# A four-mixer kernel: the delta rules' matrices, transposes and inverses put in separate stages, and gla's v projected by channel

## The chip, the cores and the metric

The kernel runs on one core of one Trainium2 chip. The metric is the device time of one execution in microseconds (us); lower is better. Times before are the median of three runs.

## The reference

One layer with x of 2048 tokens by 1024 channels. The normed x is projected to four mixers of 256 channels (4 heads of 64), whose outputs are joined, projected back, normed and added to x.

```python
h = _rmsnorm(x, pre_norm_w[l])
proj = jnp.einsum('btd,de->bte', h, w_in[l])
p_gdn, p_rwkv, p_sc, p_gla = _split(proj, [GDN_COLS, RWKV_COLS, SC_COLS, GLA_COLS])
# gdn, in chunks of 64 tokens: a delta rule, with t_mat = a_mat + I
u = lax.linalg.triangular_solve(t_mat, v * beta[..., None], ...)
w = lax.linalg.triangular_solve(t_mat, kb * jnp.exp(g)[..., None], ...)
v_new = u_c - jnp.einsum('bhck,bhkv->bhcv', w_c, s)
o = jnp.einsum('bhck,bhkv->bhcv', q_c, s) + jnp.einsum('bhij,bhjv->bhiv', attn_c, v_new)
s = s * jnp.exp(gl_c)[..., None, None] + jnp.einsum('bhck,bhcv->bhkv', k_c, v_new)
# rwkv7: also a delta rule, token by token; shortconv: a gated causal convolution
# gla, in chunks of 64: no inverse
o = jnp.einsum('bhck,bhkv->bhcv', qe_c, s) + intra_c
s = s * jnp.exp(bl_c)[..., 0, :, None] + jnp.einsum('bhck,bhcv->bhkv', ke_c, v_c)
# and at the end
out = jnp.einsum('bte,ed->btd', y, w_out[l])
x = x + _rmsnorm(out, post_norm_w[l])
```

## The kernel before, in words

The tokens are cut into 4 blocks of 512 (`NBLK`, `BL`), a block into 4 tiles of 128 (`tt`), a tile into 2 chunks of 64 (`cp`). Two tiles make a pair, so a block has two pairs of gdn (G) and two of rwkv (R): 16 pairs in all, counted by `n`.

Matmuls of the projections take operands in a high and a low part (`hh`, `hl` for the tokens, two halves of a `w` buffer for the weights), three products for each. A weight tile of 128 columns makes 24 matmuls with 512 moving columns into a PSUM bank `pp`, of which there are two. gla's v alone is projected by token: `proj_v` holds tokens still and moves 256 columns of weights, and takes both `pp` banks at once.

A pair goes through these stages. The matrices (`gdn_mats`, `rwkv_mats`, L792 and L949) make the 64 by 64 matrices of 8 chunk-heads (`Bh`, `Bl`, the high and low part), `attn` or `M4`, and also the transposed keys and values that the chain needs (`kT`, `vT`, `BKT`, `UV`). `inverse` (L580) inverts the 8 matrices together, by four levels of two groups of matmuls in the one PSUM bank `psi`, VectorE writing `W`, `X`, `Y` and the block-diagonal `Yb` between them, then a last level and a correction; the result is `Yf`. The chain (`gdn_chain`, `rwkv_chain`, L993 and L1039) carries the state over four chunks, each a string of small matmuls in `psc` with VectorE or ScalarE between. Norm, gate and store follow (`norm`, `put`); they are off the state's path. gla has a chain of its own, without an inverse.

The order is made when the kernel is recorded. Each of `chains`, `inverses`, `prepare`, the norms of the next block and `projections` is a generator; `weave` (L229) steps those that are ready by its own count of TensorE's time and the guessed latencies in `LAT`, and takes matmuls of `projections` to fill what is left. A generator waits for named events: `("B", n)` the matrices of pair n, `("I", n)` its inverse, `("C", n)` its chain, `("T", name, blk, tt)` one tile of a chain. Before the change `prepare` waits for `("I", n - 1)` before it makes the matrices of pair n, as there is one buffer each of `Bh` and `Bl`. Within an engine the chip then keeps the recorded order. The projections of rwkv of a block wait for the chain of rwkv of the block before, `("R", blk - 1)`, and those of gla for `("L", blk - 1)`, as their buffers are single. After the last block's projections come 32 output projections (two of 512 columns for each of 16 token tiles), with nothing beside them at the end.

Of the kernel before, what the change touches and what calls it, by code (L numbers as in the profile page):

```python
# [19 lines left out]
P = 128  # L20
# [25 lines left out]
CST = {"ident": 0, "dlt": 128, "cum": 256, "msi": 384, "rst": 640, "bones": 640 + BL}  # L46
NCST = 640 + BL


def make_consts():  # L50
# [10 lines left out]
    c[:, 640:NCST] = np.arange(BL) % 64 > 0  # L61
# [3 lines left out]
    m += [-((j // (2 * s) == i // (2 * s)) & (j % (2 * s) >= s) & (i % (2 * s) < s)).astype(np.float32) for s in LEVELS]  # L65
    return c, np.concatenate([x.astype(np.float16) for x in m], 1)


def layout(inp):
# [4 lines left out]
    starts += [GLA0, GLA0 + 128, GLA0 + 512, GLA0 + 640]  # L74
# [5 lines left out]
    wv = w[:, GLA0 + 256:GLA0 + 512].reshape(KT, P, 256).transpose(1, 0, 2).reshape(P, KT * 256)  # L80
# [8 lines left out]
    for nm, key in (("w0", "rwkv_w0"), ("a0", "rwkv_a0"), ("kk", "rwkv_k_k"), ("ka", "rwkv_k_a"), ("rk", "rwkv_r_k"),  # L89
# [13 lines left out]
        "wv": wv,  # L103
# [24 lines left out]
class Ring:  # L128
# [18 lines left out]
    "M4": (512, 4), "BKT": (512, 2), "UV": (512, 2),   # L147
    "ru": (256, 2), "lu": (256, 3), "or": (256, 2),  "Yf": (64 * 8, 1), "y": (256, 1),
    "t2": (BL, 4), "gk": (16, 9), "sx": (64, 1), "dr": (16, 1), "kn": (4 * TT, 3), "rB": (256, 1), "sm": (16, 14),

    "lqk": (BL, 2), "lv": (BL, 2), "lk": (128, 1), "lgz": (2 * BL, 1), "ld": (8, 1), "lg": (BL, 2), "n32": (32, 4), "gs": (TT, 2),
# [21 lines left out]
LAT = {"gates": 6.0, "ipre": 2.0, "gates2": 1.0, "norms": 3.2, "chan": 0.9, "pool": 1.38, "decay": 2.6, "mats": 2.2, "inv0": 1.0, "inv1": 2.2,  # L173
# [4 lines left out]
def h4(t):  # L178
    return t.rearrange("p (h d) -> p h d", h=4)
# [10 lines left out]
class K:  # L190
# [60 lines left out]
    def setup(self, ctx):  # L251
# [29 lines left out]
        self.rst = g("rst", BL)  # L281
        c16 = c.tile([P, 64 * (2 + len(LEVELS))], F16, name="c16")
# [187 lines left out]
    def load_half(self, blk, wi, i):  # L470
# [4 lines left out]
        if wi == "v":  # L475
            wh, wl = (t.rearrange("p (k c) -> p k c", k=2) for t in self.load_parts(blk, (wi, i), self.a["wv"][:, i * BL:(i + 1) * BL]))
            return (wh, self.hh), (wl, self.hh), (wh, self.hl)
# [3 lines left out]
    def proj(self, blk, groups):  # L481
# [3 lines left out]
        for n, (_, tiles, _) in enumerate(groups):  # L485
            nj = range(len(tiles))
            halves = [(n, j, i) for i in range(4 if tiles[0][0] == "v" else 2) for j in nj]
# [8 lines left out]
        for n, j, i, ks in work:  # L496
# [10 lines left out]
            if first:  # L507
                pss[n, j] = self.pp() if tiles[j][0] != "v" else [self.pp() for _ in range(2)]
# [3 lines left out]
            if tiles[j][0] == "v":  # L512
                yield from self.proj_v(ps, i, pairs)
                if i == 3:
                    with self.tc.high_priority(offset=PRIO):
                        tiles[j][1](ps)
                fin += 1
                continue
# [14 lines left out]
            yield 0.0  # L533

    def proj_v(self, ps, i, pairs):

        for q, (w, h) in enumerate(pairs):
            for k in range(2):
                for t in range(TT):
                    o = 256 * (t % 2)  # L540
                    self.mm(ps[t // 2][:, o:o + 256], h[:, 2 * i + k, t * P:(t + 1) * P], w[:, k, :], start=(i + q + k + t % 2 == 0),
                            stop=(i == 3 and q == 2 and k == 1), skip_group_check=True)
            yield 0.0
# [248 lines left out]
    def gdn_mats(self, tt, Bh, Bl):  # L792
# [339 lines left out]
    def prepare(self):  # L1132

        n = 0
        for blk in range(NBLK):
            for name in "GR":
# [323 lines left out]
```

## Time and profile before

| what | before |
|---|---|
| median of 3 runs (lowest, highest) | 1380.45 us (1375.13, 1382.61) |
| the profiled execution: time, span | 1379.89 us, 1378.1 us |
| TensorE busy (PE) | 1284.7 us, 93% of the span |
| VectorE busy (DVE) | 967.7 us, 70% |
| ScalarE, GpSimd busy (ACT, POOL) | 530.2 us, 355.5 us |
| mean granted TensorE clock | 0.985 |

The span runs from the first to the last instruction; the profiled execution's time is 1.8 us longer. A busy share is a mean over stages, and a small matmul counts as busy for its whole latency, about 0.2 us, though the next one can start much earlier; so TensorE at 93% is not at 93% of its peak.

### The profile page before, as it was taken

What the parts mean: (1) busy time and instruction counts of PE and PEld (TensorE: products, weight loads), DVE (VectorE), ACT (ScalarE), POOL (GpSimd) and SP (SyncE); (2) the same over time, 40 slices, a digit from 0 to 9 for tenths busy, and PEclk for the clock granted to TensorE, in tenths of its full rate; (3) what the DMA queues carried; (4) which work ended last, traced back from release to release, by engine and by line L of the source; (5) the groups of instructions that cost most, each with busy time, mean ns of one, the idle gap of its engine ahead of it and who ended that gap; (6) DMA issues with size and microseconds to landing.
All of it is one profiled execution on the core that took longest, in us unless ns stands there. A gap on an engine that the chain in (4) does not pass through costs nothing. (4 is left out here: it accounts for less than half of the span.)

```text
span 1378.1 us, 26007 instructions
## 1 busy us (share of the span) xinstructions
PE 1284.7 (93%) x10088; PEld 982.1 (71%) x10088; DVE 967.7 (70%) x2194; ACT 530.2 (38%) x1167; POOL 355.5 (26%) x437
## 2 busy tenths in 40 slices
PE   5989988899999999999999999999998998999997
PEld 3767766767667767767777677776776776677886
DVE  5766698869876895778657977888669847743232
ACT  4663454336242431425423432453224325133221
POOL 5554444201221021101301210203111135233321
PEclk9999999999999999999999999999999999999999
DMA  8776554544244424453543335432444363233442
GB/s 283 263 258 231 206 177 146 177 152 133 82 139 146 157 89 135 146 177 105 173 146 130 130 120 174 144 110 68 127 143 145 103 198 121 89 99 116 151 151 100
DMA packets 98509, 204.63 MB, mean 148 GB/s; under 512 B 9153, under 2 KB 39249, under 8 KB 98385
## 3 DMA queue, kind: packets, MB, share of 16 engines
q1 hardware_dynamic: 98384, 202.96, 44.6%
q8 instruction: 79, 1.29, 0.4%
q14 instruction: 46, 0.37, 0.1%
HBM read 153.65 MB, written 49.28 MB: 147 GB/s over the span
## 5 line engine op out<-in xcount | busy, mean ns | idle before, releaser
L199 PE MATMUL pp<-hh,w 128*128 128x512 f32 (+1 forms) x2144 | 609.6, 408 | 7.6 <-DMA w<-parts 5.9
L199 PEld LDWEIGHTS pp<-hh,w 128*128 128x128 f32 (+1 forms) x2144 | 389.8, 190 | 92.0 <-issue 4.7
L199 PE MATMUL pp<-hl,w 128*128 128x512 f32 (+1 forms) x1088 | 323.1, 408 | 2.0 <-POOL hl L435 2.0
L199 PEld LDWEIGHTS pp<-hl,w 128*128 128x128 f32 (+1 forms) x1088 | 198.2, 190 | 45.4 <-POOL hl L435 3.8
L352 POOL TENSOR_TENSOR w<-raw,w 128x512 fp32r<-128x512 f32 (+1 forms) x102 | 129.3, 1270 | 223.6 <-ACT w L351 143.0
L351 ACT CAST w<-raw 128x512 fp32r<-128x512 f32 (+1 forms) x102 | 60.3, 593 | 130.5 <-issue 56.8
L356 POOL TENSOR_TENSOR sm<-sm,mhalf 128x4 f32<-128x4 f32 (+1 forms) x64 | 59.3, 927 | 193.4 <-DVE sm L1099 148.7
L199 PE MATMUL pp<-woh,w 128*128 128x512 f32 x256 | 71.8, 401 | 0.0
L681 DVE SCALAR_TENSOR_TENSOR pq<-pq,par,pq 128x512 f32<-128x512 f32 x72 | 59.4, 826 | 11.0 <-ACT pq L678 8.5
L605 DVE COPY Yb<-Y 64x512 f16<-64x512 f16 x160 | 55.8, 349 | 2.2
L199 PEld LDWEIGHTS <-Yb 128*128 128x128 f16 x640 | 25.2, 98 | 41.5 <-issue 22.9
L199 PEld LDWEIGHTS pp<-woh,w 128*128 128x128 f32 x256 | 47.6, 191 | 9.7
L199 PE MATMUL psi<-W,Yb 128*128 128x64 f16 x640 | 32.7, 194 | 22.3 <-DVE W L613 17.5
L618 DVE TENSOR_TENSOR X<-psi,X 128x512 f16<-128x512 f32 x64 | 43.9, 686 | 12.8 <-PE psi L199 12.5
L199 PEld LDWEIGHTS <-Bb 128*128 128x128 f16 x768 | 29.8, 99 | 29.5 <-issue 23.4
L613 DVE TENSOR_TENSOR W<-psi,c 128x512 f16<-128x512 f32 x64 | 43.8, 685 | 5.9 <-PE psi L199 5.3
L1393 DVE SCALAR_TENSOR_TENSOR pq<-pq,sm,x 128x512 f32<-128x512 f32 x32 | 24.6, 769 | 30.4 <-DMA x<-in_x 19.7
L620 DVE STREAM_TRANSPOSE Y<-X 128x512 f16<-128x512 f16 x64 | 45.2, 707 | 0.7
L199 PE MATMUL psi<-X,Bb 128*128 128x64 f16 x768 | 40.0, 195 | 6.2 <-DVE X L618 4.2
L1382 ACT ACTIVATE x<-pp 128x512 f32<-128x512 f32 x32 | 19.1, 598 | 64.1 <-PE pp L199 64.1
L847 ACT COPY pq<-pp 128x512 f32<-128x512 f32 x36 | 21.1, 586 | 53.0 <-PE pp L199 53.0
L199 PE MATMUL pp<-w,hh 128*128 128x256 f32 x256 | 36.6, 289 | 0.1
(320 smaller groups left out, 2152.4 us busy)
## 6 DMA issues: line engine op xcount, KB each, us to landing
w<-parts SPq DMA_DIRECT2D x174, 512.0 KB, 3.3
parts<-w SPq DMA_DIRECT2D x58, 512.0 KB, 4.0
raw<-in_wt SPq DMA_DIRECT2D x58, 256.0 KB, 3.2
x<-in_x SPq DMA_DIRECT2D x56, 256.0 KB, 3.0
raw<-yd SPq DMA_DIRECT2D x32, 256.0 KB, 2.9
out<-pq SPq DMA_DIRECT2D x32, 256.0 KB, 2.0
x<-in_xt SPq DMA_DIRECT2D x24, 256.0 KB, 2.9
w<-parts_v SPq DMA_DIRECT2D x12, 512.0 KB, 3.3
```

What stands on the lines that cost most here:

```text
L199: return self.nc.tensor.matmul(out, w, x, **kw)
L351: self.nc.scalar.copy(hi, src)
L352: self.nc.gpsimd.tensor_tensor(lo, src, hi.bitcast(F32), ALU.subtract)
L356: self.nc.gpsimd.tensor_tensor(dst, x, self.mhalf[:, 0:x.shape[1]], ALU.pow)
L605: nc.vector.tensor_copy(Yb[hs(c), :, hs(c)], Y[hs(c)])
L613: nc.vector.tensor_tensor(W, v(ps), m4(self.lev[lv]), ALU.mult)
L618: nc.vector.tensor_tensor(X2, v(ps), X, ALU.add)
L620: nc.vector.transpose(Y, X)
L681: nc.vector.scalar_tensor_tensor(acc, p[:, i:i + BL], self.pcol("conv", 4 * ct + i), acc, ALU.mult, ALU.add)
L847: nc.scalar.copy(p[:, 1:], ps)
L1382: nc.scalar.activation(junk, ps[i], AF.Square, accum_out=ss[:, i:i + 1])
L1393: nc.vector.scalar_tensor_tensor(o, o, r, x, ALU.mult, ALU.add)
```

## The change

The matrices of a pair and the transposed keys and values that only the chain reads are now two generators' steps: `gdn_mats` and `rwkv_mats` end with the matrices, and `gdn_more` and `rwkv_more` do the rest after them, before an event `("M", n)` for which the chain waits as well. `Bh` and `Bl` have two buffers, so that `prepare` waits for the inverse of pair n - 2 instead of n - 1. `M4` has six buffers instead of four and `attn` three instead of two; the fourth tile's matrices wait for the first tile's chain, and `more` of the second pair for the same tile of the first pair.

To make room for it, `BKT` is gone (the transposed keys are copied back over `BK`, in two copies instead of one), `t2` has three buffers instead of four, `gdn_out` shares the buffer `y` with the other outputs, and the reset mask is kept in fp16. gla's v is projected like every other tile, two tiles of 128 channels, and transposed in `gla` beside the keys, so that one copy of 384 columns takes the place of one of 128. The cut diff:

```diff
--- before.py
+++ after.py
...
+    "t2": (BL, 3), "gk": (16, 9), "sx": (64, 1), "dr": (16, 1), "kn": (4 * TT, 3), "rB": (256, 1), "sm": (16, 14),
...
+    "lqk": (BL, 2), "lv": (BL, 2), "lkv": (384, 1), "lgz": (2 * BL, 1), "ld": (8, 1), "lg": (BL, 2), "n32": (32, 4), "gs": (TT, 2),
...
-    "kq": (2 * BL, 2), "gv": (BL, 2), "ggz": (2 * BL, 1), "attn": (256, 2), "kT": (256, 4), "vT": (256, 2),
-    "gu": (256, 3), "t1": (256, 3), "og": (256, 2), "gy": (256, 1),
+    "kq": (2 * BL, 2), "gv": (BL, 2), "ggz": (2 * BL, 1), "attn": (256, 3), "kT": (256, 4), "vT": (256, 2),
+    "gu": (256, 3), "t1": (256, 3), "og": (256, 2),
...
-RINGS16 = {"Bh": 1, "Bl": 1, "W": 1, "X": 2, "Y": 1}
+RINGS16 = {"Bh": 2, "Bl": 2, "W": 1, "X": 2, "Y": 1}
...
-        kT, vT = g["kT"][tt], self.R["vT"]()
-        nc.vector.tensor_tensor(h4(kT), h4(kT), bc(g["ke"]), ALU.mult)
-        ps = self.psa()
-        for pr in range(2):
-            self.tr(ps[:, pr * P:(pr + 1) * P], g["v"][pr][:, tt * P:(tt + 1) * P], self.ident)
-        nc.vector.tensor_tensor(h4(vT), h4(ps[:, 0:256]), bc(g["kv"]), ALU.mult)
...
-        return dict(attn=h4(attn), kT=kT, vT=vT)
+        return dict(attn=h4(attn))
+
+    def gdn_more(self, tt, m):
+
+        nc = self.nc
+        g = self.g
+        bc = lambda s: s[:, 4 * tt:4 * tt + 4].unsqueeze(2).to_broadcast([P, 4, 64])
+        kT, vT = g["kT"][tt], self.R["vT"]()
...
+        m.update(kT=kT, vT=vT)
+        yield 0.0
...
-            en, ak = self.t2(), self.t2()
+            en, ak, kk = self.t2(), add[:, pr, :], lw
...
-            kk = self.t2()
...
+        yield 0.0
+        return dict(M4=M4)
...
+    def rwkv_more(self, tt, m):
+
...
         ps = self.psa()
...
-        bt = self.R["BKT"]()
-        nc.scalar.copy(bt, ps)
+        for pr, bd in enumerate(bds):
...
+        for pr, bd in enumerate(bds):
+            nc.scalar.copy(bd, ps[:, 2 * P * pr:2 * P * pr + 2 * P].rearrange("p (c x) -> p c x", c=2))
...
-        return dict(M4=M4, bt=bt, uv=uv)
+        m.update(bt=bds, uv=uv)
...
-                o = (2 * cp + h // 2) * P + 64 * (h % 2)
-                self.mm(pC[hs(h % 2), hs(h // 2)], bt[:, o:o + 64], uv[:, cp, hs(h)], start=True, stop=True)
+                self.mm(pC[hs(h % 2), hs(h // 2)], bt[h // 2][:, cp, hs(h % 2)], uv[:, cp, hs(h)], start=True, stop=True)
...
-        y = self.R["gy"]()
+        y = self.R["y"]()
...
-                    if n:
-                        yield "I", n - 1
+
+                    if n > 1:
+                        yield "I", n - 2
                     B, ms = [self.R16[x]() for x in ("Bh", "Bl")], []
+                    mats, more = (self.gdn_mats, self.gdn_more) if name == "G" else (self.rwkv_mats, self.rwkv_more)
+                    for i in range(2):
+                        tt = 2 * pair + i
+                        if tt == 3:
+                            yield "T", name, blk, 0
+                        m = yield from mats(tt, *(t[:, 4 * i:4 * i + 4, :] for t in B))
+                        ms.append(m)
+                    self.mats[n] = ms, B
+                    self.done("B", n, lat=LAT["mats"])
                     for i in range(2):
                         if pair:
                             yield "T", name, blk, i
-                        m = yield from (self.gdn_mats if name == "G" else self.rwkv_mats)(2 * pair + i, *(t[:, 4 * i:4 * i + 4, :] for t in B))
-                        ms.append(m)
-                    self.mats[n] = ms, B
-                    self.done("B", n, lat=LAT["mats"])
+                        yield from more(2 * pair + i, ms[i])
+                    self.done("M", n, lat=LAT["more"])
                     n += 1
...
                         yield "I", n
+                        yield "M", n
                         ms, Y = self.mats.pop(n)
...
-        todo = [(None, ((WT_GLA + i, lambda ps, t=t: nc.scalar.copy(t, ps)),), None) for i, t in enumerate((qf, kf))]
...
-        def fv(ps):
-            for t, p in zip(v, ps):
-                nc.scalar.copy(t, p)
-        todo.append((None, (("v", fv),), None))
+        todo = [(None, ((WT_GLA + i, lambda ps, t=t: nc.scalar.copy(t, ps)),), None) for i, t in enumerate([qf, kf] + v)]
...
-        at, ke, vt = u1(), self.R["lk"](), L["v"][tt // 2][:, 256 * (tt % 2):256 * (tt % 2) + 256]
+        at, kv = u1(), self.R["lkv"]()
+        ke, vt = kv[:, 0:P], kv[:, P:]
...
         pt = self.psa()
-        self.tr(pt[:, 0:P], L["ed"][:, ts], self.ident)
-        nc.scalar.copy(ke, pt[:, 0:P])
+        for i, t in enumerate([L["ed"]] + L["v"]):
+            self.tr(pt[:, i * P:(i + 1) * P], t[:, ts], self.ident)
+        nc.scalar.copy(kv, pt[:, 0:3 * P])
         yield LAT["gA"]
...
```

On TensorE, in the last tile of block 0's rwkv chain, from its first chunk to its second (`Sr`, `ru` and `UV` are operands of the chain's matmuls, `Yf` the inverse, `BKT` or `BK` the transposed keys, `qbd` and `lg` gla's, `or` an output, `pp` the projections), the rows before, word for word:

```order
L199 MATMUL pp<-hh,w_160 128x512 x3
L199 MATMUL pp<-hh,w_158 128x512
L199 MATMUL psc<-ru_80,Yf_87 64x64 x4
L199 MATMUL pp<-hh,w_158 128x512 x3
L199 MATMUL pp<-hl,w_158 128x512 x2
L199 MATMUL psc<-UV_79,BKT_77 64x64 x4
L203 MATMUL psa<-cst,or_85 128x128 x2
L199 MATMUL psa<-qbd,lqk_123 64x256 x2
L203 MATMUL psa<-cst,lg_129 128x128
L199 MATMUL pp<-hl,w_158 128x512
L199 MATMUL psc<-Sr,AR_63 128x128
L199 MATMUL psc<-Sr,AR_64 128x128
```

and in the same tile now:

```order
L197 MATMUL pp<-hh,w_161 128x512 x4
L197 MATMUL pp<-hh,w_159 128x512 x4
L197 MATMUL psc<-ru_80,Yf_87 64x64 x4
L197 MATMUL pp<-hl,w_159 128x512 x4
L197 MATMUL pp<-hh,w_159 128x512 x4
L197 MATMUL pp<-hh,w_160 128x512
L197 MATMUL psc<-UV_79,BK_65 64x64 x2
L197 MATMUL psc<-UV_79,BK_66 64x64 x2
L197 MATMUL pp<-hh,w_160 128x512 x3
L197 MATMUL pp<-hl,w_160 128x512 x4
L197 MATMUL psc<-Sr,AR_63 128x128
L197 MATMUL psc<-Sr,AR_64 128x128
```

Between the chain's matmuls with `Sr` and `ru`, `ru` and `UV`, `UV` and `Sr` stood 4, 5 and 1 projection matmuls, and in the last place gla's first matmuls; now 8, 9 and 7 projection matmuls stand there.

On VectorE, where the inverse of the first pair of block 0 begins (`Bb`, `Y`, `X`, `Yb`, `W` are the inverse's; `t` and `attn` a gdn pair's matrices; `AR` and `BK` the rwkv projections), before:

```order
L591 COPY Bb_151<-Bh_145 64x8x64 x2
L598 TENSOR_TENSOR Y_150<-Bh_145,c_203 128x512
L801 TENSOR_TENSOR t_196<-cst,gk_93 128x256
L599 TENSOR_TENSOR Y_150<-Y_150,c_203 128x512
L802 TENSOR_TENSOR t_198<-cst,gk_97 128x256
L601 STREAM_TRANSPOSE X_148<-Y_150 128x512
L605 COPY Yb_152<-Y_150 64x8x64 x2
L381 TENSOR_TENSOR sm_118<-sm_117 128x4
L382 TENSOR_SCALAR sm_118<-sm_118 128x4
L613 TENSOR_TENSOR W_147<-psi,c_203 128x512
L852 SCALAR_TENSOR_TENSOR AR_63<-pq_138,par,pq_139 128x4x128
```

and now:

```order
L569 COPY Bb_152<-Bh_144 64x8x64 x2
L576 TENSOR_TENSOR Y_151<-Bh_144,c_204 128x512
L577 TENSOR_TENSOR Y_151<-Y_151,c_204 128x512
L785 TENSOR_TENSOR t_199<-t_199,t_200 128x256
L579 STREAM_TRANSPOSE X_149<-Y_151 128x512
L583 COPY Yb_153<-Y_151 64x8x64 x2
L591 TENSOR_TENSOR W_148<-psi,c_204 128x512
L798 TENSOR_TENSOR t_200<-psa,t_198 128x2x64
L799 TENSOR_TENSOR attn_188<-psa,t_199 128x2x64
L798 TENSOR_TENSOR t_200<-psa,t_198 128x2x64
L799 TENSOR_TENSOR attn_188<-psa,t_199 128x2x64
L596 TENSOR_TENSOR X_150<-psi,X_149 128x512
```

The second pair's matrices (`t`, `attn`), which before came after this inverse was written out, now stand between its first steps; the vT of both tiles comes in before the inverse begins. Counted in VectorE's instructions from the start, the four inverses of block 0 are written out after 167, 308, 408 and 553 before, and after 173, 314, 401 and 489 now.

## Rows read from the trace of the kernel before

**Rows 1.** The page: busy us by engine, and its TensorE and clock slices.
```profile
PE 1284.7 (93%) x10088; PEld 982.1 (71%) x10088; DVE 967.7 (70%) x2194; ACT 530.2 (38%) x1167; POOL 355.5 (26%) x437
PE   5989988899999999999999999999998998999997
```

**Rows 2.** The last-ending chain in order of time: start us, us, what.
```profile
1273.60 97.06 PE pp L199 x428
```

**Rows 3.** Stretches, projection matmuls alone: busy us (count), clock, DMA share, GB/s.
```profile
100.00:1262.00 1162.00, 824.54 (x3247) 0.99 0.43 140
180.00:260.00 80.00, 51.37 (x239) 0.96 0.45 155
340.00:420.00 80.00, 45.78 (x151) 0.98 0.38 118
680.00:900.00 220.00, 166.73 (x680) 0.99 0.43 141
```

**Rows 4.** Same stretches, all engines: PE, PEld, DVE, ACT, POOL, clock, DMA.
```profile
100.00:1262.00 1162.00, 1096.51 (x9249) 831.58 (x9249) 866.94 (x1991) 447.25 (x987) 268.47 (x342) 0.99 0.43 140
180.00:260.00 80.00, 67.61 (x579) 54.62 (x578) 68.08 (x132) 33.40 (x71) 33.77 (x29) 0.96 0.45 155
340.00:420.00 80.00, 77.78 (x831) 56.15 (x830) 63.97 (x177) 30.84 (x80) 16.42 (x24) 0.98 0.38 118
680.00:900.00 220.00, 211.17 (x1705) 162.47 (x1703) 166.84 (x369) 76.17 (x162) 31.96 (x52) 0.99 0.43 141
```

**Rows 5.** TensorE's waits: us in total, times, longest.
```profile
PE psi L199 <- DVE W L613: 17.5, 17, 4.8
PE psi L199 <- DVE X L618: 4.2, 5, 2.1
PE psa L199 <- DVE t L801: 3.5, 1, 3.5
PE psi L199 <- DVE Yb L605: 2.5, 4, 0.9
PE psi L199 <- DVE W L626: 2.1, 3, 1.0
PE psi L199 <- DVE X L601: 1.9, 2, 1.5
```

**Rows 6.** Groups by line: operation, count, busy, mean ns, idle before.
```profile
L199 PE MATMUL pp<-w,hh 128*128 128x256 f32 x256 | 36.6, 289 | 0.1
L199 PE MATMUL pp<-w,hl 128*128 128x256 f32 x128 | 18.6, 288 | 0.0
L983 ACT COPY BKT<-psa 128x512 f32<-128x512 f32 x16 | 9.3, 582 | 1.1 <-PE psa L203 0.8
L989 ACT COPY UV<-psa 64x256 f32<-64x256 f32 x32 | 11.7, 366 | 2.0 <-PE psa L203 1.6
```

**Rows 7.** TensorE's timeline: start, us, then line, operation, tiles, shapes, count.
```profile
537.60 1.08 PE L199 MATMUL pp<-hh,w 128*128 128x512 f32 x4
538.61 0.45 PE L199 MATMUL psc<-ru,Yf 64*64 64x64 f32 x8
...
553.58 1.12 PE L199 MATMUL pp<-w,hh 128*128 128x256 f32 x8
554.63 0.45 PE L199 MATMUL psc<-ru,Yf 64*64 64x64 f32 x8
...
918.48 1.09 PE L203 MATMUL psa<-cst,kq 128*128 128x128 f32 x8
919.50 0.39 PE L199 MATMUL psi<-X,Bb 128*128 128x64 f16 x8
```

**Rows 8.** Tiles: ns min, median, max of the 128-column copy and of `Yb`.
```profile
L1289 ACT COPY lk<-psa x16: 242/265/266, 372.9 to 1252.8; 128x128 f32<-128x128 f32 x16
L605 DVE COPY Yb<-Y x160: 242/291/1411, 100.6 to 1185.3; 64x512 f16<-64x512 f16 x160
```

**Rows 9.** Timelines of one stall of block 0: VectorE, GpSimd, TensorE; then the clock.
```profile
182.60 2.77 DVE L605 COPY Yb<-Y 64x512 f16<-64x512 f16 x2
187.15 0.68 DVE L613 TENSOR_TENSOR W<-psi,c 128x512 f16<-128x512 f32 x1
...
182.08 1.73 POOL L352 TENSOR_TENSOR S<-radd,S 128x512 fp32r<-128x512 f32 x1
...
187.88 0.58 PE L199 MATMUL psi<-W,Yb 128*128 128x64 f16 x8 [4.78 <-DVE W L613]
...
185.00:195.00 10.00, 7.12 (x38) 5.82 (x39) 8.92 (x16) 4.82 (x8) 1.52 (x2) 0.66 0.30 105
```

More of the change, by code (lines that the diff above doesn't have):

```diff
@@ L73, in layout @@
     starts += [SC0 + P * i for i in range(8)]
-    starts += [GLA0, GLA0 + 128, GLA0 + 512, GLA0 + 640]
+    starts += [GLA0 + P * i for i in range(6)]
     tiles = [w[:, s:s + P].reshape(KT, P, P).transpose(1, 0, 2).reshape(P, KT * P) for s in starts]
@@ L280, in setup @@
         self.strict, self.incl = self.msi[:, 0, 0:64], self.msi[:, 0, 64:128]
-        self.rst = g("rst", BL)
-        c16 = c.tile([P, 64 * (2 + len(LEVELS))], F16, name="c16")
+        c16 = c.tile([P, 64 * (2 + len(LEVELS)) + BL], F16, name="c16")
+        self.rst = c16[:, 64 * (2 + len(LEVELS)):]
         par = c.tile([P, NPAR], F32, name="par")
@@ L486, in proj @@
             nj = range(len(tiles))
-            halves = [(n, j, i) for i in range(4 if tiles[0][0] == "v" else 2) for j in nj]
+            halves = [(n, j, i) for i in range(2) for j in nj]
             order += halves
@@ L507, in proj @@
             if first:
-                pss[n, j] = self.pp() if tiles[j][0] != "v" else [self.pp() for _ in range(2)]
+                pss[n, j] = self.pp()
             if n == 0:
@@ L532, in proj @@
                     self.done("P", blk, after, lat=2.5)
[L533 to L542, printed above, removed]
             yield 0.0
@@ L829, in gdn_mats @@
         nc.gpsimd.tensor_tensor(Bl, h4(B32), Bh, ALU.subtract)
-        return dict(attn=h4(attn), kT=kT, vT=vT)
+        return dict(attn=h4(attn))
[4 more added lines that the diff above has]
+        kT, vT = g["kT"][tt], self.R["vT"]()
+        nc.vector.tensor_tensor(h4(kT), h4(kT), bc(g["ke"]), ALU.mult)
+        ps = self.psa()
+        for pr in range(2):
+            self.tr(ps[:, pr * P:(pr + 1) * P], g["v"][pr][:, tt * P:(tt + 1) * P], self.ident)
+        nc.vector.tensor_tensor(h4(vT), h4(ps[:, 0:256]), bc(g["kv"]), ALU.mult)
+        m.update(kT=kT, vT=vT)
+        yield 0.0
     def rwkv_proj(self):
@@ L971, in rwkv_mats @@
         nc.gpsimd.tensor_tensor(Bl, h4(B32), Bh, ALU.subtract)
-        for pr in range(2):
-            bd = BK[pr][:, 2 * tt:2 * tt + 2, :]
+        yield 0.0
+        return dict(M4=M4)
+    def rwkv_more(self, tt, m):
+        nc = self.nc
+        r = self.r
+        BK = r["BK"]
+        bds = [BK[pr][:, 2 * tt:2 * tt + 2, :] for pr in range(2)]
+        for pr, bd in enumerate(bds):
             for c in range(2):
@@ L977, in rwkv_mats @@
         ps = self.psa()
-        for cp in range(2):
-            for pr in range(2):
-                o = (2 * cp + pr) * P
-                self.tr(ps[:, o:o + P], BK[pr][:, 2 * tt + cp, :], self.ident)
-        bt = self.R["BKT"]()
-        nc.scalar.copy(bt, ps)
+        for pr, bd in enumerate(bds):
+            for cp in range(2):
+                o = (2 * pr + cp) * P
+                self.tr(ps[:, o:o + P], bd[:, cp], self.ident)
+        for pr, bd in enumerate(bds):
+            nc.scalar.copy(bd, ps[:, 2 * P * pr:2 * P * pr + 2 * P].rearrange("p (c x) -> p c x", c=2))
         ps = self.psa()
```

28 lines of the change are left out of this document (7 added, 21 removed).

## The prediction

> **What bounds the kernel now.** I read the page first: TensorE is busy 93% of the span, VectorE 70%, the other two far less, and the slices show no long stretch in which TensorE is free except at the very start [rows 1]. The chain of waits says the same from the other end: followed back from the last instruction it is 97.06 us of 428 projection matmuls and nothing else [rows 2], 0.227 us each. That is the price of such a matmul when nothing interrupts it. So the kernel is bound by TensorE's queue, and a stage is worth what it adds to that queue: its matmuls, and the time in which the queue stands still or crawls.
>
> How much of the middle is crawl? Between 100 and 1262 us the projections have 3247 matmuls [rows 3], 384 of them gla's v with 256 columns (counted below). All matmuls there are 9249 [rows 4], so 6002 are small ones. 2863 at 0.227 are 650 us, the 384 at 0.131 (below) 50 us; 462 us are left for the small ones, 77 ns each, with all waits and switches in it. The same sum by stage: 67 ns in 340 to 420 us (151 projections, 680 small), 73 ns in 680 to 900 us (584 projections, 96 of v, 1025 small), 103 ns in 180 to 260 us (143, 96 and 340) [rows 3, 4]. In that last stage a gdn chain, an inverse, rwkv's preparation and block 0's weight splitting meet; VectorE is busy 68.08 of 80 us there, more than in any other of these stages. So the price of a small matmul moves with how late VectorE is, not with how few projections are left: the stage poorest in projections, 340 to 420 us, is the cheapest.
>
> The waits by name: TensorE waits mostly for the inverse's VectorE steps. Six kinds of wait stand in [rows 5]; the five of them that belong to the inverse (`W`, `X`, `Yb`) sum to 28.2 us, and the wait for `t`, the first step of a gdn pair's matrices, is 3.5 us, once.
>
> **The change, part by part.** The sum is made against the profiled execution: span 1378.1 us, time 1379.9 us, 0.5 us under the median of 1380.45.
>
> gla's v. Before: 384 matmuls of 256 columns [rows 6]; eight of them take 1.05 us from 553.58 to the next row's 554.63, 0.131 us each, 50.3 us in all [rows 7]. Now: 192 matmuls of 512 columns. Four take 1.01 us between chain steps [rows 7], 0.2525 us each, 48.5 us; at the undisturbed 0.227 they would be 43.6 us. I take the price in the midst of the chains: **-1.8 us**, bound -6.7 us. The weights' bytes and loads stay the same, four halves a block.
>
> Transposes of v in gla: two more for each of 16 tiles, 32. Eight transposes of that shape take 1.02 us [rows 7], 0.1275 us each: **+4.1 us** on TensorE's queue. The copy behind them grows from 128 to 384 columns: 0.265 us for 128 [rows 8], 0.582 us for 512 [rows 6], so about 0.48, 0.2 us more, 16 times, 3.4 us. ScalarE is busy 530.2 us of the span [rows 1], and the mask of `at` on VectorE runs beside it; I take 0, bound +3.4 us.
>
> `BKT`'s copy in two: 0.582 us becomes about two of 0.366 [rows 6], 0.15 us more for each of 16 tiles, on ScalarE and now before the event `M`, not before the inverse: 0, bound +2.4 us. The new wait for `M` has only the chain's own next matmul behind it. If the chain comes first, that matmul stops TensorE's whole queue. But `M` is recorded while the inverse still has levels to go, so I take 0.
>
> Shorter rings: `y` shared by all outputs, `t2` with three buffers. The cover is the distance between outputs, as tiles of one chain follow each other through four chunk steps, and an output's write is one of 16 for each mixer in the whole run. I take 0; if a write met an unfinished store, the VectorE queue would stand behind it. Fp16 mask: the same scan, 0.
>
> The decoupling itself. It removes no instruction. It lets a pair's matrices stand between another inverse's steps, takes the scaling of `kT`, the copies and transposes of `vT`, `BK`, `UV` out of what the inverse waits for, and, as the order of VectorE shows, brings the fourth inverse of block 0 forward by 64 instructions (553 to 489). At VectorE's mean of 0.44 us (967.7 us over 2194 [rows 1]) that is 28 us of VectorE work. But the first three come out after 173, 314 and 401, against 167, 308 and 408: nothing is won there. What is won is filling: in the last tile of rwkv 8, 9 and 7 projection matmuls stand where 4, 5 and 1 stood, each worth about 0.25 us.
>
> What is that worth? Below: nothing, if the filling only moves from one place to another, as every projection put here is missing elsewhere. Above: all 6002 small matmuls at the best stage's 67 ns instead of 77, 57 us. Between: at the price of 680 to 900 us, 73 ns, it would be 23 us. By the waits: 28.2 us of the inverse and 3.5 us for `t`. I take the whole of the 3.5, since the matrices no longer wait for the inverse ahead, and two fifths of the 28.2, as one inverse in four moves clearly and the others have another pair's matrices around them: 11.4. Together **-15 us**, which is 2.5 ns for each small matmul, well inside the bound.
>
> The sum: 1379.9 - 1.8 + 4.1 - 15 = 1367.2. **I predict 1367 us.**
>
> **Rivals.** A measurement of this kernel tells about 0.5%, 6.9 us, from no change: faster is under 1373.5, slower over 1387.4.
>
> *More is won.* If all waits of the inverse and for `t` go, 31.7 us, the time is 1379.9 - 1.8 + 4.1 - 31.7 = 1350.5. With them some of the low clock would go: after the stall of 4.78 us at 183 us, the granted clock of 185 to 195 us is 0.66 [rows 9], that is, part of this stretch ran at 1.2 GHz and the rest at 2.4; a third of 10 us, 3.4 us, was lost to one stall. Five of that size would give 1350.5 - 17 = 1334. For it speaks that the waits are many and short; against it, that VectorE has no instruction less. The Trainium skill, "TensorE: Matmul & The Clock Gate", section "HAM oscillation — how this bites in real kernels", has it that idle gaps of TensorE are paid twice, by the gap and by a slow clock after it. The trace agrees at this stall, with its 0.66.
>
> *Nothing is won.* VectorE does the same work in the same total, 967.7 us [rows 1], and where the stages meet it was already late. The filling moves and the waits move with it. Then only v and the transposes count: 1379.9 + 2.3 = 1382. For it speaks that the cheapest stage was the one with fewest projections, and that three inverses of four come no earlier.
>
> *Slower.* Three things now run together, a chain, an inverse and another pair's matrices, and VectorE becomes the bound where it was near it. The place is the middle of each block, from the second gdn pair to the first rwkv pair, as in 180 to 260 us, with VectorE 0.85 busy [rows 4]. One wait there took 4.78 us: two `Yb` copies took 2.77 us instead of twice the median 0.291 [rows 8], and `W` came last behind them; GpSimd ran a 1.73 us subtraction at the time [rows 9]. If each of the 16 inverses loses 2.5 us more, 40 us, less the 12.7 won in the sum above, the time is 1379.9 + 40 - 12.7 = 1407; at 2 us it is 1399. It decides from (12.7 + 6.9) / 16 = 1.2 us for each inverse. Against it: only block 0 splits weights on GpSimd, which is busy 31.96 of 220 us later on [rows 4]. The Trainium skill, "SBUF — State Buffer", section "Who interferes with whom", says that a copy of VectorE in a two-port mode and a GpSimd instruction exclude each other for a whole instruction, which speaks against putting more of the inverse beside GpSimd's work. The stretched `Yb` copies agree with it.
>
> **How the numbers follow.** The forecast, 1358 to 1373 us, has 0.40. More won, under 1358, has 0.15. Nothing won, 1373.5 to 1387, has 0.27: the order's evidence for three inverses of four. Slower has 0.18. So faster 0.55, same 0.27, slower 0.18. The range leaves out the outer half of both end cases: from 1346 (the 1350.5 of all waits gone, with v at its bound of -6.7) to 1390, just past the bound of no change with the copies' 3.4 and 2.4 us on the path (1388). The likeliest case alone goes from 1358 to 1373.
>
> **What the profile will show.** If the steps are right: TensorE's waits for `W`, `X` and `Yb` sum to some 17 us instead of 28.2, the wait for `t` is gone, TensorE's busy time falls less than the span does, and the undisturbed run of projections at the end is longer than 97 us by the filling that was not needed earlier, with the same 0.227 us each. 192 more projection matmuls of 512 columns and 32 more transposes of `lv` stand there, with ScalarE's copy at 0.45 to 0.5 us. It is wrong if the waits for VectorE keep their sum under other names (chain steps `gu`, `UV`, `Sg`), which gives 1382, or if TensorE waits for the tiles of `more`, or for a `y` whose store has not landed. It is wrong on the far side if VectorE is over 0.95 busy in the middle of every block.

## The result and the profile after

The changed kernel takes 1388.0 us (median of 20 runs, 1376.9 to 1394.8), the kernel before 1379.1 us (20 runs beside it, 1373.7 to 1383.1). The ratio is 1.0061, 95% interval 1.0046 to 1.0077: 0.6% slower, where 1.0% faster was forecast (1367 of 1380.45). The profiled execution took 1384.26 us, its span is 1382.4 us. Ratios below leave out runs over 1.5% above the fastest of their kernel, which are three of e2's twelve (with them e2 is at 1.0041).

The page's engines and TensorE's slices, as [rows 1]:

```profile
PE 1283.9 (93%) x9928; PEld 976.0 (71%) x9928; DVE 955.6 (69%) x2194; ACT 529.4 (38%) x1181; POOL 355.0 (26%) x437
PE   5979878999989999999999898999998998999997
```

The last link of the last-ending chain (start, us, what, count), as [rows 2]:

```profile
1257.94 117.00 PE pp L197 x516
```

TensorE is busy as long as before and idle 5 us longer (1382.4 - 1283.9 = 98.5 against 93.4). The undisturbed run of projections at the end grew from 97 to 117 us, at the same 0.227 us each. So the middle needed less filling, as forecast, but it ended only 15.7 us sooner (1257.94 against 1273.60) for the 20 us of filling that it left to the end. Stretches, projections alone (as [rows 3]), then all engines (as [rows 4]):

```profile
100.00:1262.00 1162.00, 820.43 (x3045) 0.99 0.43 140
...
100.00:1262.00 1162.00, 1095.93 (x9083) 825.96 (x9083) 857.41 (x1997) 445.81 (x998) 268.38 (x342) 0.99 0.43 140
180.00:260.00 80.00, 68.76 (x577) 52.40 (x575) 72.14 (x150) 33.53 (x76) 30.91 (x26) 0.91 0.39 136
```

The small matmuls cost (1162 - 3045 x 0.227) / 6038 = 78.0 ns each, against 77: the 2.5 ns that the forecast wanted are not there. In 180 to 260 us VectorE is busy 72 of 80 us, more than before, and the clock fell to 0.91. TensorE's waits, as [rows 5] (us in total, times, longest):

```profile
PE psi L197 <- DVE W L591: 20.8, 18, 2.9
PE psi L197 <- DVE X L579: 9.3, 7, 1.9
PE psa L197 <- DVE t L779: 3.8, 2, 2.8
PE psa L197 <- DVE W L604: 3.5, 4, 1.4
PE psi L197 <- DVE Yb L583: 3.4, 6, 1.3
PE psi L197 <- DVE X L596: 2.1, 4, 1.3
PE psi L197 <- DVE X L613: 1.4, 4, 0.4
```

The six kinds of the inverse sum to 40.5 us; all such kinds of before, two short ones more than [rows 5] shows, sum to 30.4. The wait for `t` is still there. X L579 is the inverse's start (X L601 before, 1.9 us): TensorE now comes to it before VectorE has. These waits are not what the time follows: in the run e1 below, 1.2% faster, the waits of the inverse still sum to 35.9 us, the two largest being

```profile
PE psi L197 <- DVE W L591: 19.9, 17, 4.1
PE psi L197 <- DVE X L579: 6.6, 5, 2.1
```

The timelines of VectorE at the end of the same inverse, that of block 3's second gdn pair, show what the overlap does to an inverse. First the changed kernel, then e1, in which a pair's matrices are held for the inverse ahead:

```profile
1070.61 0.67 DVE L613 TENSOR_TENSOR X<-psi,X 128x512 f16<-128x512 f32 x1
...
1073.00 0.68 DVE L949 TENSOR_TENSOR M<-psa,cst 128x512 f32<-128x512 f32 x1
...
1074.37 0.67 DVE L627 TENSOR_TENSOR W<-X,psi 128x512 f16<-128x512 f16 x1
...
1075.05 1.18 DVE L953 TENSOR_TENSOR rB<-M,kn 64x128 f32<-64x128 f32 x4
1076.25 1.29 DVE L949 TENSOR_TENSOR M<-psa,cst 128x512 f32<-128x512 f32 x2
1077.53 1.19 DVE L953 TENSOR_TENSOR rB<-M,kn 64x128 f32<-64x128 f32 x4
...
1079.35 0.68 DVE L636 TENSOR_TENSOR Yf<-psi,Y 128x512 f32<-128x512 f32 x1
```

```profile
1050.46 0.68 DVE L613 TENSOR_TENSOR X<-psi,X 128x512 f16<-128x512 f32 x1
...
1052.94 0.68 DVE L627 TENSOR_TENSOR W<-X,psi 128x512 f16<-128x512 f16 x1
...
1053.62 0.68 DVE L949 TENSOR_TENSOR M<-psa,cst 128x512 f32<-128x512 f32 x1
...
1055.00 0.69 DVE L636 TENSOR_TENSOR Yf<-psi,Y 128x512 f32<-128x512 f32 x1 [0.62 <-PE psi L197]
1055.68 0.58 DVE L953 TENSOR_TENSOR rB<-M,kn 64x128 f32<-64x128 f32 x2
```

In the changed kernel the first rwkv pair's `M` and `rB` stand between the correction's last steps, and from X to Yf it takes 8.7 us. In e1, with one `M` ahead of `Yf`, it takes 4.5, and there VectorE waits for TensorE (0.62 us, in brackets); in the kernel before it takes 4.8. Over all 16 inverses, from TensorE's first matmul to the end of `Yf`, the mean is 36.7 us in the changed kernel, 35.1 in e1 and 35.3 before.

**The clock differs too.** Each run has its granted clock. Over its 20 runs the changed kernel's mean is 0.9828; over 34 runs beside the first four experiments the kernel before has 0.9893. Time multiplied by clock, which takes one lost per cent of clock as one lost per cent of time, is 1362.8 us for the one and 1362.9 for the other. By that measure the whole loss is clock, but it takes too much off. By a straight line through the changed kernel's runs 0.01 of clock goes with 11.2 us, through those of the kernel before with 8.3, not 14 (in other kernels with anything from 0, e11, to 14, e1); by the first two 2 to 4 of the 9 us are left at one and the same clock, and the two profiled executions, both at 0.985, differ by 4.4 us. So some 5 to 7 of the 9 us go with the clock, and whether the clock or the order behind it is the cause is not shown. The experiments are told in both measures. The kernel before, taken again beside each group of them (e1 to e4, e5 to e8, e9 to e12, e13 to e15, e16 and e17), has 1362.9, 1360.3, 1361.3, 1360.8 and 1355.5 us in time x clock (1360.5 without one run that took 1372.87 us at 0.951), so that a difference of under 3 us between groups says nothing.

### The profile page after: what moved, and what is told of

The parts are those of the page before. It is cut to its first block, busy times and chain, and to the rows that moved or that the text cites. A ratio compares the mean times of both kernels' runs of the same rounds, so it can differ in the third digit from the quotient of the medians.

```text
span 1382.4 us, 25708 instructions
## 1 busy us (share of the span) xinstructions
PE 1283.9 (93%) x9928; PEld 976.0 (71%) x9928; DVE 955.6 (69%) x2194; ACT 529.4 (38%) x1181; POOL 355.0 (26%) x437
## 4 chain that ended last, share of the span: by engine, by line
PE 52%; DVE 18%; issue 4%; POOL 3%; ACT 3%; DMA 2%; SPq 0%; POOLq 0%; ACTq 0%; DVEq 0%
PE pp L197 39%; PE psc L197 6%; PE psa L197 3%; PE psi L197 2%; PE psa L201 2%; POOL sm L354 2%; DVE Yb L583 1%; DMA x<-in_xt 1%; DVE X L596 1%; DVE W L591 1%; DVE Y L598 1%; DVE t L879 0%; DVE AR L895 0%; DVE M L949 0%; DVE og L1023 0%
## 5 line engine op out<-in xcount | busy, mean ns | idle before, releaser
L197 PE MATMUL pp<-hh,w 128*128 128x512 f32 (+1 forms) x2272 | 646.0, 408 | 5.3 <-DMA w<-parts 3.2
L197 PEld LDWEIGHTS pp<-hh,w 128*128 128x128 f32 (+1 forms) x2272 | 412.0, 190 | 90.6 <-DMA w<-parts 4.1
L197 PE MATMUL pp<-hl,w 128*128 128x512 f32 (+1 forms) x1152 | 342.7, 410 | 2.0 <-POOL hl L433 2.0
L197 PEld LDWEIGHTS pp<-hl,w 128*128 128x128 f32 (+1 forms) x1152 | 210.8, 191 | 47.7 <-POOL hl L433 3.8
L1009 ACT COPY gu<-psc 64x128 f32<-64x128 f32 x64 | 16.6, 259 | 58.7 <-PE psc L197 57.4
## 6 DMA issues: line engine op xcount, KB each, us to landing
raw<-in_wt SPq DMA_DIRECT2D x62, 256.0 KB, 3.1
x<-in_x SPq DMA_DIRECT2D x56, 256.0 KB, 3.0
raw<-yd SPq DMA_DIRECT2D x32, 256.0 KB, 2.9
out<-pq SPq DMA_DIRECT2D x32, 256.0 KB, 2.3
x<-in_xt SPq DMA_DIRECT2D x24, 256.0 KB, 3.2
```

Of the source, the lines that this page charges most:

```text
L197: return self.nc.tensor.matmul(out, w, x, **kw)
```

## The experiments

Kernels against before, 4 to 12 compared runs each (the changed kernel 20; time x clock of before from the first group):

| kernel | ratio, 95% interval | mean clock | time x clock |
|---|---|---|---|
| before | 1 | 0.9893 | 1362.9 |
| changed | 1.0061 [1.0046, 1.0077] | 0.9828 | 1362.8 |
| e1 hold all | 0.9941 [0.9914, 0.9968] | 0.9882 | 1353.4 |
| e2 hold first rwkv pair | 1.0018 [0.9990, 1.0046] | 0.9887 | 1364.0 |
| e3 changed, v by token | 1.0053 [1.0034, 1.0071] | 0.9825 | 1360.9 |
| e4 before, v by channel | 1.0011 [0.9992, 1.0029] | 0.9857 | 1358.9 |
| e5 rest first | 1.0021 [1.0005, 1.0037] | 0.9884 | 1363.3 |
| e6 hold all, rest first | 1.0024 [1.0006, 1.0041] | 0.9794 | 1351.7 |
| e7 hold all, v by token | 0.9899 [0.9865, 0.9934] | 0.9905 | 1351.4 |
| e8 hold second gdn pair | 1.0074 [1.0049, 1.0099] | 0.9797 | 1358.8 |
| e9 e7, waiting for the chain | 1.0015 [0.9996, 1.0035] | 0.9853 | 1359.0 |
| e10 changed, more slack | 1.0108 [1.0077, 1.0139] | 0.9780 | 1360.9 |
| e11 e7, more slack | 0.9957 [0.9940, 0.9973] | 0.9861 | 1351.2 |
| e12 hold second rwkv pair | 1.0053 [1.0035, 1.0070] | 0.9849 | 1362.2 |
| e13, e14 pads, misplaced | 1.0292, 1.0287 | 0.976, 0.977 | 1381.1, 1382.2 |
| e15 e7, one wait less | 1.0003 [0.9993, 1.0014] | 0.9842 | 1354.9 |
| e16 e7, pads in the inverse | 1.0122 [1.0099, 1.0144] | 0.9868 | 1375.0 |
| e17 e7, pads behind it | 1.0093 [1.0067, 1.0120] | 0.9777 | 1359.3 |

**e1: the overlap undone.**

```diff
-                    if n > 1:
-                        yield "I", n - 2
+                    if n:
+                        yield "I", n - 1
```

> The changed kernel with one edit: a pair's matrices wait for the inverse just ahead again, as in the kernel before, so no matrices stand between the steps of another inverse. The split of matrices and the rest, the rings, and v by channel stay. Theory A, the bunch (in the middle of each block the second gdn pair's inverse, the first rwkv pair's matrices and a chain now fall on VectorE together, and TensorE waits): the loss of 8.9 us (ratio 1.0061) goes, down to the sum of v and the transposes, 1.000 to 1.002 of before; the stretches without projections behind the second gdn inverse, 12 to 14 us in each block, go too. Theory B, v by channel is the loss (384 matmuls of 256 columns against 192 of 512 and 32 transposes): the time stays at 1.005 to 1.007. Theory C, the moved rest (the copies and transposes behind the event M) is the loss: it stays at 1.005 or above.

Theory A's direction, and more than its size: not 1.000 but 0.9941. The overlap costs 1.2% of the time, 16.5 us (9.4 us in time x clock), and what is left of the change wins 0.6%. The inverses of block 0 start at 103.5, 163.2, 225.2 and 282.3 us; with the overlap at 103.6, 162.8, 219.8 and 282.2. So matrices that are ready sooner start one inverse of these four sooner, by 5 us, and that one also ends later, at 262.5 instead of 256.0 us. The time is lost from one block to the next: the fourth inverse of block 0 ends at 316.7 us with the overlap and 317.3 without, but the first of block 1 starts at 400.3 instead of 390.8, that of block 2 at 694.9 instead of 674.2, that of block 3 at 976.8 instead of 956.4. From the first start to the last end in a block the overlap saves 1 to 6 us, but fewer projections go in there (516 instead of 544 in block 0) and have to be made behind it. Theory A's other sign did not come: around the second gdn inverse the longest gap between projections is 7.1 to 8.8 us with the overlap and still 5.4 to 8.1 without.

**e2, e8, e12: one pair of each block held** (the same line, for one pair only).

> The changed kernel with one edit: only the first rwkv pair of each block waits for the inverse just ahead of it; the other pairs keep the overlap. Theory A, the bunch in the middle of each block: this one wait takes the bunch away and the wins at the block's ends remain, so the time is 0.995 to 1.000 of before, under that of the kernel in which all pairs wait. If the overlap costs the same at each pair, it is a quarter of the way: 1.0045. Theory B and C (v by channel, the moved rest): 1.005 to 1.007, as the changed kernel.

> The changed kernel in which only the second gdn pair of each block waits for the inverse ahead of it; the other three keep the overlap. If the loss is shared by the four pairs evenly, a quarter of 1.2% comes back: 1.003. If it sits in the inverse of the second gdn pair (its inverses last 43 to 51 us with the overlap and 40 to 48 without): this pair's matrices are not the ones that stand in that inverse, they stand in the first pair's, so nothing comes back, 1.005 to 1.007. If it sits between the two gdn pairs, 0.997 to 1.000.

> The changed kernel in which only the second rwkv pair of each block waits for the inverse ahead. Holding the first rwkv pair brought nothing in time multiplied by clock (1363 us as 1363), holding the second gdn pair 4 us (1359), holding all four 9.4 us (1353). If the shares add, the second rwkv pair and the first gdn pair have the 5.9 us left: here 1357 to 1360 us in time multiplied by clock, 1.000 to 1.005 of before in time. If only all together count, 1361 to 1363, 1.005 to 1.008.

In time x clock, holding the first rwkv pair, where I had looked for the whole loss, brings nothing (1364.0), the second rwkv pair 0.6 us, the second gdn pair 4.0; all together 9.4. In time, 0.4% and 0.1% come back in the first two and nothing in the third, whose clock is lowest; e12 is what was expected if only all together count. So none of these three places holds the loss, and Theory A's "middle of each block" is too narrow; the first gdn pair was not held alone.

**e3, e4: v by channel.** e3 is the changed kernel with the old `proj_v`, `wv` and the 128-column copy; e4 is the kernel before with the new ones.

> The changed kernel with gla's v projected by token as before (384 matmuls of 256 columns, no transposes of v, the copy of 128 columns). Theory A, the bunch: by the sum of the prediction, 2.3 us less than the changed kernel, 1.004 to 1.0045 of before; at most 4 us less. Theory B, v by channel is the loss: 1.000 or below.

> The kernel before with gla's v by channel alone (192 matmuls of 512 columns, 32 transposes of v, the copy of 384 columns, the shared y). Theory A: the sum of the prediction, +2.3 us, 1.0017 of before; between 0.9985 (the matmuls at 0.227 us each) and 1.004 (the copy on the path too). Theory B: the whole loss, 1.006.

Theory B is out: undone in the changed kernel, v gives back 0.1% in time, 1.9 us in time x clock. Alone in the kernel before it changes the time by 0.1%, inside its interval. The sum's +2.3 fits but is not resolved: in time x clock v by channel costs 1.9 us in the one kernel and saves 4.0 in the other (1358.9 against 1362.9 beside it).

**e5, e6: the split undone,** with the overlap and without: the rest of a pair comes ahead of the event that the inverse waits for.

```diff
-                    self.done("B", n, lat=LAT["mats"])
                     for i in range(2):
                         if pair:
                             yield "T", name, blk, i
                         yield from more(2 * pair + i, ms[i])
+                    self.done("B", n, lat=LAT["mats"])
```

> The changed kernel with the split undone and the overlap kept: the rest of a pair (scaling and transposes of kT, vT, BK, UV and their copies) is issued before the event B that the inverse waits for, as before, and not after it. Theory D (what the first runs leave: the split wins, the overlap loses; the inverses are paced by the chains and so do not use matrices that are ready sooner): the split's win of 7 to 9 us is gone and the overlap's loss is still there, 1.010 to 1.014 of before. Rival E (split and overlap only hurt together, as the rest of one pair then falls into the inverse of another): 0.998 to 1.003.

> The changed kernel with split and overlap both undone; v by channel, the rings of the change and the order of the transposes stay. Theory D: nothing is left of win or loss, 0.999 to 1.003, as the kernel before with v by channel (1.0011). If the rings or the transposes' new form count, it departs from that by over 0.3%.

e6 came as Theory D said, e5 did not: in time the overlap costs nothing without the split (1.0021 and 1.0024) and 1.2% with it. That is Rival E by the ratios. In time x clock it is no interaction: the overlap costs 11.6 us without the split (1363.3 and 1351.7) and 9.4 with it. The two views differ by the clock, 0.9794 in e6 and 0.9884 in e5, which by that measure is 28 and 16 us of 1380; the times are 1380.1 and 1379.3. No run here says which view is right.

**e7: the split alone, v by token.** The edits of e1 and e3.

> Split alone: the changed kernel with the overlap undone (each pair's matrices wait for the inverse ahead) and gla's v by token as before. Theory D: the split alone wins 0.6%, and v counts by at most 0.1% either way: 0.992 to 0.996 of before. By the sum of the prediction v by token saves 2.3 us more: 0.9925. If v by channel is what won in the run that holds all pairs, this one is back at 0.998 to 1.001.

0.9899, the lowest ratio here, 1.0% under the kernel before and a little under Theory D's range; its interval overlaps e1's. v by channel is not what won in e1.

**e9: e7, waiting for the chain again.**

```diff
-                        if tt == 3:
-                            yield "T", name, blk, 0
+                        if pair:
+                            yield "T", name, blk, i
```

> The split alone (each pair's matrices wait for the inverse ahead, v by token: 0.9899 of before), in which a second pair's matrices wait for the chain again as before, its first tile for the chain's first tile and its second for the second; the change has only its second tile wait for the first. Theory F (the win is that the inverse of a second pair no longer stands behind the chain of the first): its inverses start some 15 us later in each block, and the win goes, 0.998 to 1.002. Rival G (the win is that the inverse waits for less work, the rest being issued after B): it stays at 0.988 to 0.993.

Theory F: the win goes, 1.0015 (7.6 us in time x clock, the rest clock). The second inverse of block 0 starts at 176.5 instead of 163.1 us, the fourth at 316.9 instead of 283.3. By this run, what won was that a second pair's inverse does not stand behind the chain of the first; e15 below goes against it. In e6, where the rest waits for the chain and holds the inverse, the time is back at 1.0024 too, though not time x clock.

**e10, e11: more slack,** in the changed kernel and in e7.

```diff
-"ipre": 2.0, ... "inv0": 1.0, "inv1": 2.2,
+"ipre": 3.0, ... "inv0": 2.0, "inv1": 3.2,
```

> The changed kernel with three numbers of the planner's table larger by 1 us (ipre 2 to 3, inv0 1 to 2, inv1 2.2 to 3.2): it takes an inverse's steps to be ready later, and puts more projections between them. Theory H (with another pair's matrices between an inverse's steps, VectorE's answer comes later than the table says; TensorE reaches the next step too soon and stands): the waits for W, X and Yb fall from 40 us to under 20, and the time to 0.993 to 1.000. Rival I (VectorE is the bound in the middle of the blocks, so TensorE stands whatever is put there): the waits keep over 30 us, the inverses end later, and the time stays at 1.006 to 1.012.

> The same three numbers in the kernel with the split alone and v by token (0.9899 of before). It is the control for the run above: if the numbers were too small without the overlap too, this gains as much as that one, to 0.980 to 0.985; by theory H alone, with no other pair's matrices between the steps, little is to be had and each inverse comes later, 0.988 to 0.994.

The waits fell nearly as Theory H said, to 22.5 us and not under 20; the time did what Rival I said, so neither holds. The waits of e10:

```profile
PE psi L197 <- DVE W L591: 9.0, 8, 2.7
PE psi L197 <- DVE W L604: 5.6, 3, 3.8
PE psi L197 <- DVE X L579: 2.6, 3, 2.1
PE psi L197 <- DVE W L627: 2.5, 1, 2.5
PE psi L197 <- DVE X L613: 1.9, 2, 1.0
PE psi L197 <- DVE X L596: 0.9, 1, 0.9
```

Time x clock falls by 1.9 us only, while the time rises by 0.5%. In e7 the slack moves time x clock by 0.2 us and the time by 0.6%, outside the range expected. So the sum of TensorE's waits in the inverse is no measure of what they cost: projections put there are missing elsewhere (the run of them at the end falls from 516 to 428), and an inverse takes 7 to 8 us longer in the mean.

**e13, e14, e16, e17: VectorE's price, inside the inverse and behind it.** 12 idle multiplications for each pair, between the inverse's steps or ahead of the next pair's matrices. In e13 and e14 they read only their own spare tile:

> The split alone with v by token (0.9899 of before, 1351 us in time multiplied by clock) with idle work on VectorE added between the steps of each inverse: 12 multiplications of a spare tile of 256 columns by itself, 0.42 to 0.45 us each, 5.2 us for each of 16 inverses, about what a pair's matrices take on VectorE. Nothing reads the tile. Theory J (VectorE being late between an inverse's steps is what the overlap costs): 8 to 14 us more in time multiplied by clock, 1359 to 1365, and 0.996 to 1.004 in time. Rival L (the price is not VectorE's but lies in the order of TensorE's or ScalarE's work): at most 3 us more, 0.989 to 0.994.

> The same 12 multiplications for each pair, six ahead of each tile's matrices, which come behind the inverse and beside the chain's first steps. Theory J: little, 0 to 4 us more in time multiplied by clock, 0.989 to 0.994. Rival K (VectorE's sum counts, wherever it stands): as much as the run above. Rival L: as little as the run above.

Both put them into the first block. VectorE's slices on the page of e7, without them:

```profile
DVE  5776799697765997777668885876669967543323
```

of e13:

```profile
DVE  8999999899776699687865996867669967633322
```

and of e14:

```profile
DVE  8999999998776698687865996777659967543222
```

So these runs say nothing on the place. In e16 and e17 each reads a tile of its place:

```diff
             yield LAT["inv0"]
+            self.spare(1, W[:, 0:4, :].rearrange("p u i -> p (u i)"))
...
             yield LAT["inv0"] if lv == 3 else LAT["inv1"]
+            self.spare(2, Y[:, 0:4, :].rearrange("p u i -> p (u i)"))
```

> The split alone with v by token (0.9899 of before, 1351 us in time multiplied by clock) with 12 idle multiplications of 256 columns on VectorE between the steps of each inverse, one behind each W and two behind each Y, reading that tile, so that they stay there; nothing reads what they write. About 0.43 us each, 5.2 us for an inverse, as much as a pair's matrices take on VectorE, 83 us in all. Theory J (VectorE's lateness between an inverse's steps is what the overlap costs): 8 to 14 us more in time multiplied by clock, 1359 to 1365, 0.996 to 1.004 in time. Rival K (VectorE's sum counts, wherever it stands; the front-loaded runs lost 30 us in that measure): 20 us more or above, 1.005 to 1.03. Rival L (not VectorE): at most 3 us more.

> The same 12 multiplications, for 15 of the 16 pairs, six ahead of each tile's matrices, reading the inverse just ended, so that they stand behind it and beside the chain's first steps. Theory J: 0 to 4 us more in time multiplied by clock, 0.989 to 0.994. Rival K: as much as the run above. Rival L: as little as the run above.

The groups by line of e16 (count, busy us, mean ns, idle before):

```profile
L1188 DVE TENSOR_TENSOR pad<-Y 128x256 f32<-128x256 f16 x128 | 65.4, 511 | 1.5
L1188 DVE TENSOR_TENSOR pad<-W 128x256 f32<-128x256 f16 x64 | 31.2, 488 | 0.9
```

and of e17:

```profile
L1189 DVE TENSOR_TENSOR pad<-Yf 128x256 f32<-128x256 f32 x180 | 86.5, 481 | 3.4
```

In time, the work costs 2.2% inside the inverse and 1.9% behind it, 0.32 and 0.31 us for each us of it: that is Rival K. In time x clock, 96.6 us of VectorE's work inside the inverse cost 23.6 us (0.24 us for each), 86.5 us behind it 7.9 (0.09): Theory J has the order right there, and both sizes are above its ranges. The traces bear out that much of it: an inverse takes 38.3 us in the mean in e16 and 35.4 in e17, against 35.3 in e7. A pair's matrices are about 5 us of VectorE (by e7's groups of `t` and `attn`, or of `M` and `rB`); moved from behind the inverse into it, 16 times 5 at 0.24 - 0.09 are 12 us, an estimate in time x clock, where the overlap costs 9 to 12. In time the place is worth nothing in these two runs, so that VectorE's lateness accounts for the overlap's 1.2% only if the clock is counted apart; that is argued, not shown.

**e15: one wait less.** e7 without `yield "T"` for gdn and a fourth buffer of `attn`.

> The split alone with v by token, in which a second gdn pair's second tile doesn't wait for the chain's first tile either (a fourth buffer for attn); the rwkv pairs keep that wait. By theory F (an inverse that doesn't stand behind the chain is the win) the four inverses of the second gdn pairs come some 2 to 5 us sooner: 0.985 to 0.990. If the chain's first tile is done by then anyway, no change, 0.988 to 0.993.

A miss: 1.0003 instead of 0.9899, 3.5 us of it in time x clock. The inverses of the second gdn pairs, counted from the first of their block, come 1.3 to 2.3 us sooner in three blocks and 2.7 us later in the first. One wait less thus loses in time nearly as much as e9's wait put back, so that part of e9's loss may be the order and its clock, and Theory F is supported, not shown; why e15 loses, no run here shows.

## Why the prediction was wrong

**gla's v and the transposes, +2.3:** nothing speaks against it, but it is too small to be resolved. The wider copy takes 0.478 us, as worked out (0.48); e3 and e4 put v within 0.1% in time, inside their intervals.

**Rings, `y`, the mask, the wait for `M` at nothing:** no wait of TensorE for the tiles behind `M` (`vT`, `UV`, `BK`) or for `y` is among its longer ones, and e6, which keeps all of these, is at 1.0024.

**The decoupling, -15: the step that failed.** I took it from the inverse's waits, two fifths of 28.2 us (11.3, not the 11.4 written) and the whole of 3.5, and took both halves of the decoupling for one. With the 2.3 of v taken off the 8.9 us of loss, the term measures +6.6. The runs show two edits of opposite sign. The split, with which a second pair need not wait for the chain's tiles, brings 0.6 to 1.0% (e1, e7), gone when the wait is put back (e9). The overlap, by which a pair's matrices may stand beside the inverse ahead, costs 1.2% on top of the split (e1 against the changed kernel); without the split it costs nothing in time (e5, e6). Through what the overlap costs that, VectorE or the clock or both, stays open. The 64 instructions by which the fourth inverse comes forward were read rightly, but they belong to the first half: in block 0 its end comes at 316.7 us instead of 354.8, and at 317.3 without the overlap. And the waits were the wrong ledger: e10 nearly halves them and wins nothing, and e1 beats the kernel before with more of them (35.9 us against 30.4).

**"Nothing is won"** named what happened to the waits: they moved and grew. 1382 is near the result by accident; two effects of 8 to 17 us lie under it. That the stated range, to 1390, takes in 1388 is luck of the same kind: its upper end came from this rival.

**"Slower"** came nearest: VectorE is late where an inverse and another pair's matrices meet. By its formula the result, 8.9 us over before, is (8.9 + 12.7) / 16 = 1.35 us for each inverse, not 2 to 2.5, just past the 1.2 from which it decides; the inverses of the traces are 1.4 us longer than before, 1.6 longer than in e1. That each such us costs a us is still its assumption. Its sign, VectorE over 0.95 busy in the middle of every block, came in two of four: 490 to 520 and 780 to 810 us, in blocks 1 and 2 (clock, DMA share and GB/s follow; the third line is the kernel before, which has such a stretch too):

```profile
490.00:520.00 30.00, 29.11 (x73) 0.94 0.23 78
780.00:810.00 30.00, 29.24 (x71) 1.00 0.24 80
...
470.00:500.00 30.00, 29.18 (x69) 1.00 0.32 102
```

Its 0.18 was too low: that VectorE has no instruction less and that three inverses of four come no earlier stood in the prediction, and speak for it as much as for "nothing is won".

**The clock** stood in the prediction only as an extra of "more is won". One stretch shows it near the crowded VectorE: three pieces around the end of block 3's second inverse, all engines, then clock:

```profile
1058.00:1068.00 10.00, 9.08 (x56) 7.11 (x54) 9.80 (x17) 3.11 (x5) 3.07 (x2) 1.00 0.53 184
1068.00:1078.00 10.00, 8.32 (x102) 6.47 (x101) 9.85 (x31) 4.85 (x14) 2.12 (x3) 0.81 0.24 80
1078.00:1088.00 10.00, 9.35 (x69) 7.40 (x68) 7.43 (x18) 6.00 (x17) 2.27 (x2) 0.85 0.17 52
```

Between 1068 and 1074 us VectorE is full, nearly all matmuls are small and TensorE stands 1.7 us in gaps of under 0.6 us, all at a granted clock of 1.00; from 1074 to 1080 TensorE is busy throughout and the clock is 0.50 to 0.54, which is 1.2 GHz. The Trainium skill, "TensorE: Matmul & The Clock Gate", section "HAM oscillation — how this bites in real kernels", has idle gaps paid a second time by the slow clock behind them. This stretch agrees in that order, though each of its gaps is short; the sums do not: e10 has 18 us less of the inverse's waits and a lower clock, 0.9780 against 0.9828. What sets a kernel's mean clock, between 0.978 and 0.9905 in kernels that differ by the order of their instructions, stays open.

## What to carry to other kernels

Before a stage is let loose, ask which of its waits the next step truly stands behind: here most inverses started hardly sooner for having their matrices sooner, and only one of two relaxations won. Try the relaxations one by one, since a sum of both hides that they differ in sign. Do not cost such a move by the bottleneck's waits, which move when they are filled; ask what work it puts between the steps of a chain on the engine that answers. Where the clock is granted run by run, read the time and the clock apart, and take the price of the clock from runs of one kernel: in the two kernels with the most runs it was 8 to 11 us for 0.01, not the 14 of a plain product.

## What the hardware showed unexpectedly

Kernels of nearly one set of instructions keep their own clock, and the time need not follow it: e5 and e6 differ by one wait and have 0.9884 and 0.9794, the means of 12 runs each, with 0.0004 and 0.0009 as the means' standard errors, at 1379.3 and 1380.1 us.

A short VectorE instruction can stretch beside GpSimd. In the changed kernel one on 16 columns takes 0.16 us (start 1065.95, first row) and the like one begun during a GpSimd instruction 1.15:

```profile
1065.95 0.16 DVE L359 TENSOR_SCALAR n<-n 128x16 int32<-128x16 int32 x1
1066.19 1.28 POOL L930 TENSOR_TENSOR radd<-radd,rgz 128x512 f32<-128x512 f32 x1 [3.81 <-ACT radd L929]
1066.36 1.15 DVE L360 TENSOR_SCALAR n<-n 128x16 int32<-128x16 int32 x1
```

It ends where that does, at 1067.5, and the inverse's next steps on VectorE, `Y` and `W`, stand behind it. The Trainium skill, "SBUF — State Buffer", section "Who interferes with whom", has it that a VectorE instruction of this kind, in a two-port mode, and a GpSimd instruction exclude each other for a whole instruction; the rows agree.
